# A hybrid decoder step: the decode rows' products with their states and memory values as plain f32 on four 32-column groups, in place of two-part products

## The chip, the cores and the metric

One Trainium2 chip, one of its eight cores. The metric is the device time of one execution in microseconds (us), from runs of the program on the chip; lower is better. A profile is one further execution taken by the hardware profiler, which lists every instruction of the five engines (TensorE as PE, with its weight loads apart as PEld, VectorE as DVE, ScalarE as ACT, GpSimd as POOL, SyncE as SP, whose queue issues most transfers) with its start and its length.

## The reference, cut to what matters

One layer of a decoder trunk for two groups of rows that share all weights: 1024 prompt tokens, and 8 decode rows (one token each) that come with a state. Three mixers read the same normalised stream: an mLSTM, a pooling mixer and an attention to a memory of 256 rows. Everything is f32.

```python
# mLSTM, decode rows: 8 rows x 4 heads, each with a matrix memory C of 256 x 256
num = einsum('btsh,bshd->bthd', s, vc) + inter[..., None] * einsum('bthd,bhde->bthe', qc, C)
C_new = decay[..., None, None] * C + einsum('bshd,bshe->bhde', kw, vc)
...
# attention to the memory, decode rows: each row has its own 256 keys and values per head
s = einsum('blhd,bmhd->bhlm', q, mk) * 256 ** -0.5
p = softmax(s)
o = einsum('bhlm,bmhd->blhd', p, mv)
```

For each of the 8 decode rows and 4 heads there is a product of one row q (1 x 256) with C (256 x 256), and one of the softmax row p (1 x 256) with the row's own values mv (256 x 256). These 64 small products are what the change is about. Nothing is shared between them, so each state and each block of values goes through TensorE once.

## The kernel before, in words

**Precision.** The large products (prompt and decode rows together, 1032 columns) are made in `float32r`, a form of f32 that TensorE multiplies with fewer bits. To keep f32 accuracy, each factor is split in two parts, hi and lo, of 12 bits each: ACT copies it to hi, DVE (or POOL) subtracts hi from it to get lo, and three products (hi·hi, lo·hi, hi·lo) are added in PSUM. `split_part` (L174 to L181) does this for weights, `halves` (L656 to L663) for data; `product` (L665 to L670) makes the three products.

**Order of the work.** Nothing is scheduled by a tool: the order in which the Python code emits instructions is the order on each engine. `run_units` (L186 to L268) goes through a list of units, one for 128 output features, each with three chunks of 384, 384 and 264 token columns (`CHUNKS`); every matmul of it comes from L250. After each 0.6 us (`GRAIN`) of its estimate of such matmuls it splits the next weights (`tick`) and lets the side work advance (`Side.advance`). Side work stands in two lanes of generators; a generator yields the time, in us of large products, that should pass before its next step. So small products are put into the stream of large ones, and the amount of large work between a step that prepares an operand and the step that multiplies it is set by a `yield`.

**Buffers.** `H(...)` takes one of 21 SBUF tiles of 128 x 1032 f32, used in rotation, for nearly all rows and loads; `K1(...)` one of 9 smaller ones; `PS()` one of 5 PSUM banks.

**The state products** are `g_sample_mlstm` (L791 on), in lane 1. There are 16 steps `j`, each with two decode rows `b`, `b + 1` of head `h = j // 4`. A step:
- `load_C(j + 1)` issues the next two states (256 KB each) on SP, and every second time the values `vb`;
- `halves` splits the two states here into two `Ch` tiles: two ACT copies (L659) and two DVE subtractions (L660) of 128 x 512;
- `yield 2.0`;
- 8 matmuls at L878 into one PSUM tile `pq`. The stationary operand is a block of 40 columns of `Qm`, zero but for the decode row's own column: column b holds q's hi part, column 32 + b its lo part. The moving operand is 256 columns of the state's hi or lo part. (2 rows) x (2 halves `k` of the 256 rows) x (2 parts) makes 8;
- the new state: for each row and half an ACT product (L884) and a DVE multiply-add in place on the state `ct` (L885), then two stores on SP (L888);
- after a head's fourth step, rows 0-7 and 32-39 of `pq` are added (L891, L892) and stored into `qC`, and `fill` (L835) puts the next head's q into `Qm`.

**The memory products** are `g_sample_xattn(h)` (L1017 on), one per head, also in lane 1. The scores are made on DVE (L1048) row by row. The softmax is transposed (L1065) and put into `Pm`, with its two parts, in blocks of 16 columns (L1068, L1069). Then, in a loop of 5, two decode rows at a time: `halves` splits the values `tiles[4 + j]` (`ck`) into two `Ch` tiles, `yield 2.0`, and 8 matmuls at L1086 into `po`. The result is copied (L1089), transposed (L1093) and its two parts are added (L1095, L1098).

**Where they lie.** The state steps are put among the large products of the query projection and the output gates, and among the prompt's attention (`g_xattn`, lane 0); the four heads of memory products follow, up to the products with `w_x_out`.

Of the kernel before, what the change touches and what calls it, by code (L numbers as in the profile page):

```python
# [15 lines left out]
T = 1024  # L16
# [14 lines left out]
# Weights are loaded up to EARLY pieces ahead at the start; each piece is split in PARTS steps, not closer  # L31
# together than SHARE of a unit's length, nor sooner than AGE after its load.
# [4 lines left out]
# Time, in us, between two looks at the side work.  # L37
# [51 lines left out]
class Split:  # L89
    """Weights, k-tiles of 128 rows and some columns, as two parts of 12 bits each, whose sum is the weight."""  # L90
# [16 lines left out]
def tile_hybrid_step(ctx: ExitStack, tc: tile.TileContext, x_prompt, mem_prompt, x_sample, cache_mem_k,  # L107
# [43 lines left out]
    # The tensor engine's clock rises after some microseconds of work: until the first loads are here.  # L151
# [9 lines left out]
    # ---------------------------------------------------------------- dense products  # L161
# [11 lines left out]
    def split_part(s, k):  # L173
        """One of the PARTS shares of the k-tiles."""  # L174
# [8 lines left out]
    def run_units(first_loads):  # L183
# [10 lines left out]
        def load_more(first=0):  # L194
            """Loads as far as the buffers reach."""
            while len(here) < len(order):
                n = len(here)
                s = order[n]
                if n < first or n < min(split + 2, free + NW + 1) or s.early and n < split + EARLY:
                    load(s)  # L200
                    here[n] = clock
                else:
                    break

        def tick(us, force=False):
            """Splits, a part at a time, as far as the buffers of the units before reach."""
# [67 lines left out]
    def weight_pairs(w2d, c0, ncols, k0=0, nk=8):  # L274
        """[(Split, column)] for each 128 columns of w2d[k0*128:, c0:c0+ncols]."""
# [12 lines left out]
    # ---------------------------------------------------------------- vectors as columns  # L288
# [59 lines left out]
    # ---------------------------------------------------------------- layer norms  # L348
# [5 lines left out]
    def ln_stats(parts, n):  # L354
        """Mean and 1/deviation of the rows that parts hold side by side."""
# [21 lines left out]
    def to_features(rows, c0, n, g0, b0, wait, per=1):  # L377
        """Transposes normalised rows of one chunk, applies gain and offset, splits into xhi, xlo."""
# [15 lines left out]
    def g_rows_in():  # L394
        """x, normalised, by token."""
# [26 lines left out]
    # ================================================================ phase 1: memory keys and values  # L422
# [43 lines left out]
    def g_kv_rows():  # L466
        """Keys and values by memory row, for the outputs and as the second factor of the attention."""
# [46 lines left out]
    # ================================================================ phase 2: gates of the mLSTM  # L514
    # Per token of a tile: a, exp(-m), exp weight of the state, decay; by head. Tile 8: decode rows.
# [10 lines left out]
    class GateSplit:  # L526
        """Both parts of the gates' weights side by side, each multiplied with both parts of x."""
# [20 lines left out]
    def g_gates():  # L548
# [19 lines left out]
        # b: sum of lf within a tile of 128 tokens; mt: running max.  # L568
# [56 lines left out]
    # ================================================================ phase 3: mLSTM  # L625
# [30 lines left out]
    def halves(hi, lo, src, scale=None):  # L656
        """src, scaled by a column, as two parts of 12 bits each."""
# [7 lines left out]
    def product(out, w, x, first=True, last=True):  # L665
        """out (+)= w^T x, both in two parts."""
# [124 lines left out]
    def g_sample_mlstm():  # L791
        """The decode rows: one step of the recurrence for each of the 32 states."""
# [900 lines left out]
```

## Time and profile before

| | us |
|---|---|
| median of 3 runs | 2214.84 |
| lowest and highest run | 2213.61, 2218.53 |
| span of the profiled execution, first to last instruction | 2210.3 |
| PE busy | 2169.0 |
| DVE busy | 1207.6 |
| ACT busy | 826.1 |
| POOL busy | 364.5 |

The profiled execution has no time of its own beside its span. How to read the views: a matmul's record is longer than the time by which it holds up the next one, since matmuls run one into the other; the cost of a matmul in a stream is the distance from its start to the next start. The shape `128*40 128x256` is 128 rows of a stationary operand with 40 columns, and a moving operand of 256 columns. In a timeline, "x8" is eight instructions merged in one row. What stands in brackets, or behind the second bar, is the time in which the engine had nothing running before the instruction, and what ended it. A group of the kind "who waited for it" lists the engines that stood idle until an instruction on the named tile was done.

### The profile page before, as it was taken

To read this page: it belongs to the slowest core of one execution; us is meant where nothing else is said; L and a number is where in the kernel's file an instruction comes from. 1 tells how busy PE (TensorE), PEld (TensorE's weight loads), DVE (VectorE), ACT (ScalarE), POOL (GpSimd) and SP (SyncE) were. 2 spreads that over 40 slices of the span, in tenths; PEclk is the share of its full clock that TensorE was granted. 3 is DMA by queue.
4 is the path that set the end of the run, shared out by engine and by line. 5 is a ranking of instruction groups with operands and counts; after the bars stand their busy time and mean duration, and the time that the engine had idled before them with its cause. 6 is when DMAs were issued, how large, how long until landed. Compare 5 with 4: busy or idle time off the path is not lost.

```text
span 2210.3 us, 36109 instructions
## 1 busy us (share of the span) xinstructions
PE 2169.0 (98%) x14337; PEld 2140.7 (97%) x14337; DVE 1207.6 (55%) x2776; ACT 826.1 (37%) x1635; POOL 364.5 (16%) x523
## 2 busy tenths in 40 slices
PE   8999999999999999999999999999999999999996
PEld 7899999999999999999999999999999999999996
DVE  6834738383767765635335556644544343443457
ACT  4524343434457543442213333444142341423421
POOL 6301010101110000211004734101010010101104
PEclk9999999999999999999999999999999999999998
DMA  9131232223367664649653223311111111111112
GB/s 264 55 106 53 58 72 53 63 61 70 90 187 260 193 193 159 217 173 339 189 165 103 87 77 86 87 49 49 42 45 49 49 49 48 39 52 45 49 49 77
DMA packets 267795, 229.50 MB, mean 104 GB/s; under 512 B 15669, under 2 KB 245863, under 8 KB 267611
## 3 DMA queue, kind: packets, MB, share of 16 engines
q1 hardware_dynamic: 261291, 208.12, 31.4%
q0 software_dynamic: 6336, 19.09, 2.3%
q8 instruction: 112, 1.84, 0.3%
q14 instruction: 56, 0.46, 0.1%
HBM read 177.13 MB, written 50.64 MB: 103 GB/s over the span
## 4 chain that ended last, share of the span: by engine, by line
PE 88%; DVE 4%; issue 3%; DMA 1%; SPq 1%; ACT 1%; POOL 1%; ACTq 0%; DVEq 0%; POOLq 0%
PE pd L250 79%; PE ps L668 1%; PE ps L669 1%; PE ps L670 1%; DMA Cs<-in_state_C_dram 1%; SPq L171 1%; DVE xlo L387 1%; PE ps L692 1%; PE ps L1086 1%; PE ps L878 1%; PE ps L382 0%; DVE st L358 0%; DVE xhi L386 0%; DVE wlo L181 0%; PE ps L688 0%
## 5 line engine op out<-in xcount | busy, mean ns | idle before, releaser
L250 PE MATMUL pd<-xhi,whi 128*128 128x384 f32 (+1 forms) x2784 | 897.3, 322 | 0.6 <-ACT gf L541 0.6
L250 PE MATMUL pd<-xlo,whi 128*128 128x384 f32 (+1 forms) x2784 | 895.0, 321 | 0.0
L250 PE MATMUL pd<-xhi,wlo 128*128 128x384 f32 (+1 forms) x2784 | 891.2, 320 | 0.0
L250 PEld LDWEIGHTS pd<-xhi,whi 128*128 128x128 f32 x2784 | 524.5, 188 | 1.9 <-ACT gf L541 0.8
L250 PEld LDWEIGHTS pd<-xlo,whi 128*128 128x128 f32 x2784 | 524.9, 189 | 0.1
L250 PEld LDWEIGHTS pd<-xhi,wlo 128*128 128x128 f32 x2784 | 524.3, 188 | 0.0
L181 DVE TENSOR_TENSOR wlo<-raw,whi 128x512 fp32r<-128x512 f32 (+1 forms) x326 | 227.0, 730 | 437.2 <-ACT whi L180 430.6
L180 ACT ACTIVATE whi<-raw 128x512 fp32r<-128x512 f32 (+1 forms) x382 | 219.4, 620 | 271.6 <-PE pd L250 201.4
L1490 ACT ACTIVATE hup<-pd 128x384 f32<-128x384 f32 (+1 forms) x132 | 60.4, 458 | 277.9 <-PE pd L250 277.7
L1503 DVE SCALAR_TENSOR_TENSOR cv<-hup,colB,cv 128x1023 f32<-128x1023 f32 x88 | 112.7, 1281 | 1.6
L1544 DVE TENSOR_TENSOR z<-pd,z 128x384 f32<-128x384 f32 (+3 forms) x120 | 59.5, 511 | 82.6 <-PE pd L250 82.6
L1500 POOL COPY tl<-hup 128x10 f32<-128x10 f32 x44 | 8.4, 192 | 519.6 <-ACT hup L1490 519.6
L366 POOL TENSOR_TENSOR rs<-rs,half 128x1 f32<-128x1 f32 (+2 forms) x60 | 38.0, 633 | 340.2 <-DVE rs L365 330.1
L1491 ACT ACTIVATE cv<-pd,colB 128x384 f32<-128x384 f32 (+1 forms) x132 | 83.6, 633 | 0.0
L181 POOL TENSOR_TENSOR wlo<-raw,whi 128x512 fp32r<-128x512 f32 x56 | 76.3, 1386 | 41.4 <-ACT whi L180 41.4
L1117 POOL DMA_DIRECT2D gD<-ch x60 | 32.8, 547 | 293.5 <-ACT ch L1116 274.4
L1509 POOL TENSOR_TENSOR cv<-cv,cv 128x1032 f32<-128x1032 f32 x22 | 53.1, 2414 | 112.6 <-DVE cv L1503 97.0
L250 PE MATMUL pd<-mh,whi 128*128 128x392 f32 (+2 forms) x192 | 62.7, 326 | 0.6 <-ACT mh L1338 0.6
L250 PE MATMUL pd<-ml,whi 128*128 128x392 f32 (+2 forms) x192 | 61.8, 322 | 0.1
L250 PE MATMUL pd<-mh,wlo 128*128 128x392 f32 (+2 forms) x192 | 61.5, 321 | 0.0
L1116 ACT ACTIVATE ch<-pd,colA 128x384 f32<-128x384 f32 (+1 forms) x60 | 32.7, 545 | 67.1 <-PE pd L250 56.2
L662 ACT ACTIVATE hh<-ps,colA 128x128 fp32r<-128x128 f32 x64 | 23.1, 360 | 79.7 <-DVE hh L663 75.0
(731 smaller groups left out, 4040.9 us busy)
## 6 DMA issues: line engine op xcount, KB each, us to landing
raw<-in_w_in_dram SPq DMA_DIRECT2D x72, 512.0 KB
raw<-in_w_up_dram SPq DMA_DIRECT2D x44, 512.0 KB
raw<-in_w_down_dram SPq DMA_DIRECT2D x22, 512.0 KB
raw<-in_w_o_dram SPq DMA_DIRECT2D x18, 512.0 KB
mx<-mixD SPq DMA_DIRECT2D x16, 516.0 KB
raw<-in_w_mem_kv_dram SPq DMA_DIRECT2D x16, 512.0 KB
Cs<-in_state_C_dram SPq DMA_DIRECT2D x32, 256.0 KB
out_dram<-Cs SPq DMA_DIRECT2D x32, 256.0 KB
```

Source lines behind the costliest of these rows:

```text
L180: nc.scalar.activation(s.hi[:, ks], s.raw[:, ks], AF.Copy)
L181: (nc.gpsimd if s.pool else nc.vector).tensor_sub(s.lo[:, ks], s.raw[:, ks], raw_f(s.hi[:, ks]))
L250: nc.tensor.matmul(p[:u.m, :n], lhsT=a, rhs=b, start=j == 0, stop=j == len(seq) - 1)
L366: nc.gpsimd.tensor_tensor(out=rs[:n], in0=rs[:n], in1=half[:n], op=OP.pow)
L662: nc.scalar.activation(hi, src, AF.Copy, scale=scale)
L1116: nc.scalar.activation(t[:, :n], p[:, :n], AF.Identity, bias=bias)
L1117: nc.gpsimd.dma_start(GD[b][f][:, c0:c0 + n], t[:, :n])
L1490: nc.scalar.activation(rw[:, c0:c0 + n], p[:, :n], AF.Copy)
L1491: nc.scalar.activation(cc[:, c0:c0 + n], p[:, :n], AF.Identity, bias=colB[:, 132 + ft:133 + ft], scale=colB[:, 88 + ft:89 + ft])
L1503: nc.vector.scalar_tensor_tensor(a, b[0], b[1], a, op0=OP.mult, op1=OP.add)
L1509: nc.gpsimd.tensor_mul(cc, CA.pop(j), cc)
L1544: nc.vector.tensor_add(Z2[f][:, cs], p[:, :n], Z2[f][:, cs])
```

## The change

Both kinds of small product are made from the f32 values themselves, with no parts.

- A step takes the decode rows `r` and `r + 4` (`i` = 0, 1) in place of two neighbours.
- Its four products (2 rows x 2 halves `k`) are plain f32 matmuls with a stationary operand of 4 columns, each zero but for the row's own. Each writes to 4 PSUM rows of its own, at 32 * (2 i + k): 0, 32, 64 and 96. A matmul's PSUM rows are the columns of the array that it uses, so the four stand on four groups of 32 columns. Over the four steps of a head each group adds up its own half of 4 decode rows.
- The moving operand is the loaded state or the loaded values, read directly: the `Ch` tiles and their splits are gone, and the DVE update of the state in place comes after the matmuls that read it.
- The halves `k` are added at the end: an ACT copy and a DVE addition of 4 rows, twice, where there was one of 8 rows (states), or a DVE copy of 16 rows (values). The transposes of the values' result are four of 4 rows in place of two of 16.
- `Qm` and `Pm` shrink to 64 columns, and lose the subtractions that made the lo parts. The values `vb` come by two transfers in place of one. The loop of the memory products has 4 passes in place of 5.
- All else is the same; the other lines of the diff take out comments.

The core of the diff:

```diff
-        Qt = H("Qm", F32R)
-        nc.gpsimd.memset(raw_f(Qt), 0.0)
-        Qm = Qt[:, :640].rearrange("p (k b j) -> p k b j", k=2, b=8)
+        Qt = H("Qm")
+        nc.gpsimd.memset(Qt[:, :64], 0.0)
+        Qm = Qt[:, :64].rearrange("p (k i x) -> p k i x", k=2, i=2)
 
         def fill(h):
             for k in range(2):
-                q = smpT[:, 0, k, h * 8:(h + 1) * 8]
-                hi, lo = Qt[:, k * 320:k * 320 + 288:41], Qt[:, k * 320 + 32:(k + 1) * 320:41]
-                nc.vector.tensor_copy(hi, q)
-                nc.vector.tensor_sub(lo, q, raw_f(hi))
+                nc.vector.tensor_copy(Qm[:, k, :, 0:16:5],
+                                      smpT[:, 0, k, h * 8:(h + 1) * 8].rearrange("p (i r) -> p i r", i=2))
...
-            h, b = j // 4, 2 * (j % 4)
+            h, r = divmod(j, 4)
             ct = Ct.pop(j)
-            if b == 0:
+            if r == 0:
                 pq = PS()
-            parts = []
+            yield 2.0
+            for k in range(2):
+                for i in range(2):
+                    o = 32 * (2 * i + k)
+                    nc.tensor.matmul(pq[o:o + 4, :256], lhsT=Qm[:, k, i, 4 * r:4 * r + 4], rhs=ct[:, i, k],
+                                     start=r == 0, stop=r == 3)
             for i in range(2):
-                t = H("Ch", F32R)
-                t = [t[:, p * 512:(p + 1) * 512].rearrange("p (k v) -> p k v", k=2) for p in range(2)]
-                halves(*t, ct[:, i])
-                parts.append(t)
-            yield 2.0
-            for i in range(2):
-                for k in range(2):
-                    for x in range(2):
-                        nc.tensor.matmul(pq[0:40, :256], lhsT=Qm[:, k, b + i], rhs=parts[i][x][:, k],
-                                         start=b + i + k + x == 0, stop=b + i == 7 and k + x == 2)
...
-            if b == 6:
-                t = K1(8)
-                nc.scalar.activation(t, pq[32:40, :256], AF.Copy)
-                nc.vector.tensor_add(t, pq[0:8, :256], t)
-                nc.sync.dma_start(qC[h * 8:(h + 1) * 8], t)
+            if r == 3:
+                for i in range(2):
+                    t = K1(4)
+                    nc.scalar.activation(t, pq[64 * i + 32:64 * i + 36, :256], AF.Copy)
+                    nc.vector.tensor_add(t, pq[64 * i:64 * i + 4, :256], t)
+                    nc.sync.dma_start(qC[h * 8 + 4 * i:h * 8 + 4 * i + 4], t)
...
-        for j in range(5):
-            parts = []
-            if j < 4:
-                if j < 2:
-                    load(cache_mem_v, j + 2)
+        for j in range(4):
+            if j < 2:
+                load(cache_mem_v, j + 2)
+            yield 2.0
+            for m in range(2):
                 for i in range(2):
-                    t = H("Ch", F32R)
-                    t = [t[:, x * 512:(x + 1) * 512].rearrange("p (m v) -> p m v", m=2) for x in range(2)]
-                    halves(*t, tiles[4 + j][:, i])
-                    parts.append(t)
-            yield 2.0
-            for i, t in enumerate(parts):
-                b = 2 * j + i
-                for m in range(2):
-                    for x in range(2):
-                        nc.tensor.matmul(po[0:16, :256], lhsT=Pm[:, m, b * 16:(b + 1) * 16], rhs=t[x][:, m],
-                                         start=b + m + x == 0, stop=b == 7 and m + x == 2)
-        o16 = K1(16)
-        nc.vector.tensor_copy(o16, po[0:16, :256])
+                    o = 32 * (2 * i + m)
+                    nc.tensor.matmul(po[o:o + 4, :256], lhsT=Pm[:, m, i, 4 * j:4 * j + 4], rhs=tiles[4 + j][:, i, m],
+                                     start=j == 0, stop=j == 3)
+        tiles.clear()
+        o4 = []
+        for i in range(2):
+            t = K1(4)
+            nc.scalar.activation(t, po[64 * i + 32:64 * i + 36, :256], AF.Copy)
+            nc.vector.tensor_add(t, po[64 * i:64 * i + 4, :256], t)
+            o4.append(t)
```

TensorE's order at the third state step, in the kernel before (L250 are large products into `pd`, L878 the state products, a row for each of the two decode rows' four):

```order
L250 MATMUL pd_7771<-xlo,whi_7411 128x384
L250 MATMUL pd_7771<-xhi,wlo_7412 128x384
L878 MATMUL ps_7577<-Ch_7759,Qm_6502 40x256 x4
L878 MATMUL ps_7577<-Ch_7762,Qm_6502 40x256 x4
L250 MATMUL pd_7771<-xhi,whi_7411 128x384
L250 MATMUL pd_7771<-xlo,whi_7411 128x384
```

And in the changed kernel, where the state products stand at L873:

```order
L250 MATMUL pd_7745<-xlo,whi_7409 128x384
L250 MATMUL pd_7745<-xhi,wlo_7410 128x384
L873 MATMUL ps_7576<-Cs_7643,Qm_6502 4x256 x4
L250 MATMUL pd_7745<-xhi,whi_7409 128x384
L250 MATMUL pd_7745<-xlo,whi_7409 128x384
```

The four stand at the place of the eight, between the same two large products, and read the loaded state `Cs` in place of its parts `Ch`.

VectorE's order at the same step, before (L660 makes the lo parts `Ch` of the state, L181 those of the next weights; L968 to L976 is the prompt's softmax and its split of the next queries, L885 the state's update):

```order
L660 TENSOR_TENSOR Ch_7759<-Cs_7654,Ch_7759 128x512
L660 TENSOR_TENSOR Ch_7762<-Cs_7654,Ch_7762 128x512
L181 TENSOR_TENSOR wlo_7768<-raw_7556,whi_7767 128x512 x2
L968 TENSOR_REDUCE mx_7790<-ps_7782 128x1
L969 TENSOR_SCALAR mx_7790<-mx_7790 128x1
L953 CAST k_1359_7794<-xq_1067_6223 128x128
L954 TENSOR_TENSOR k_1359_7794<-xq_1067_6223,k_1359_7794 128x128
L953 CAST k_1360_7797<-xq_1106_6429 128x128
L954 TENSOR_TENSOR k_1360_7797<-xq_1106_6429,k_1360_7797 128x128
L975 RECIPROCAL mx_7688<-mx_7688 128x1
L976 TENSOR_SCALAR k_1337_7687<-k_1337_7687,mx_7688 128x256
L885 SCALAR_TENSOR_TENSOR Cs_7654<-Cs_7654,decS,k_1361_7814 128x256
```

And changed (L964 to L972 the same softmax and split, L880 the update):

```order
L181 TENSOR_TENSOR wlo_7742<-raw_7555,whi_7741 128x512 x2
L964 TENSOR_REDUCE mx_7764<-ps_7756 128x1
L965 TENSOR_SCALAR mx_7764<-mx_7764 128x1
L949 CAST k_1353_7768<-xq_1067_6223 128x128
L950 TENSOR_TENSOR k_1353_7768<-xq_1067_6223,k_1353_7768 128x128
L949 CAST k_1354_7771<-xq_1106_6429 128x128
L950 TENSOR_TENSOR k_1354_7771<-xq_1106_6429,k_1354_7771 128x128
L971 RECIPROCAL mx_7672<-mx_7672 128x1
L972 TENSOR_SCALAR k_1333_7671<-k_1333_7671,mx_7672 128x256
L880 SCALAR_TENSOR_TENSOR Cs_7643<-Cs_7643,decS,k_1355_7784 128x256
```

The two `Ch` rows are gone; the update stands where it stood, behind the same softmax, and now also waits for the matmuls that read the state.

More of the change, by code (lines that the diff above doesn't have):

```diff
@@ L880, in g_sample_mlstm @@
-            for i in range(2):
-                r = 2 * j + i
+            yield 2.0
[4 more added lines that the diff above has]
+                                     start=r == 0, stop=r == 3)
+            for i in range(2):
+                x = 8 * h + r + 4 * i
                 for k in range(2):
                     t = K1()
-                    nc.scalar.activation(t, vb[j // 2][:, r % 4], AF.Copy, scale=kwT[:, k, r:r + 1])
-                    nc.vector.scalar_tensor_tensor(ct[:, i, k], ct[:, i, k], decS[:, r:r + 1], t, op0=OP.mult,
+                    nc.scalar.activation(t, vb[j // 2][:, 2 * i + r % 2], AF.Copy, scale=kwT[:, k, x:x + 1])
+                    nc.vector.scalar_tensor_tensor(ct[:, i, k], ct[:, i, k], decS[:, x:x + 1], t, op0=OP.mult,
@@ L1012, in g_xattn @@
             yield 2.2
-    Pm = cp.tile([128, 2, 128], F32R, name="Pm")
+    Pm = cp.tile([128, 2, 2, 16], F32, name="Pm")
     def g_sample_xattn(h):
@@ L1044, in g_sample_xattn @@
             for i in range(2):
[L1045 removed]
+                b = j + 4 * i
                 for m in range(2):
                     scr = K1()
[L1048 removed]
+                    nc.vector.scalar_tensor_tensor(scr, t[:, i, m], 1.0, qb[i][:, j], op0=OP.mult,
                                                    op1=OP.mult, accum_out=sc[:, m, b:b + 1])
@@ L1066, in g_sample_xattn @@
         for m in range(2):
[L1067 to L1069 removed]
+            nc.vector.tensor_copy(Pm[:, m, :, 0:16:5], p[:, m * 8:(m + 1) * 8].rearrange("p (i r) -> p i r", i=2))
         po = PS()
[L1071 to L1089 removed]
+        for j in range(4):
[3 more added lines that the diff above has]
+            for m in range(2):
+                for i in range(2):
+                    o = 32 * (2 * i + m)
[3 more added lines that the diff above has]
+        o4 = []
+        for i in range(2):
+            t = K1(4)
+            nc.scalar.activation(t, po[64 * i + 32:64 * i + 36, :256], AF.Copy)
+            nc.vector.tensor_add(t, po[64 * i:64 * i + 4, :256], t)
+            o4.append(t)
         yield 2.0
@@ L1092, in g_sample_xattn @@
         for k in range(2):
-            nc.tensor.transpose(p[:, k * 16:(k + 1) * 16], o16[:, k * 128:(k + 1) * 128], ident[:16, :16])
-        q = sp.tile([128, 2, 16], F32, tag="ot", name=nm("ot"))
-        nc.vector.tensor_copy(q, p[:, :32].rearrange("p (k c) -> p k c", k=2))
+            for i in range(2):
+                nc.tensor.transpose(p[:, k * 8 + 4 * i:k * 8 + 4 * i + 4], o4[i][:, k * 128:(k + 1) * 128], ident[:4, :4])
         for k in range(2):
             a, b = OT[h][k]
-            nc.vector.tensor_add(q[:, k, 0:8], q[:, k, 0:8], q[:, k, 8:16])
-            nc.vector.tensor_copy(a[:, T:], q[:, k, 0:8])
-            nc.vector.tensor_sub(b[:, T:], q[:, k, 0:8], raw_f(a[:, T:]))
+            nc.vector.tensor_copy(a[:, T:], p[:, k * 8:k * 8 + 8])
+            nc.vector.tensor_sub(b[:, T:], p[:, k * 8:k * 8 + 8], raw_f(a[:, T:]))
         yield 1.0
@@ L1180, in tile_hybrid_step @@
     xq_units(0)
-    on(units[n0], "before", lambda: (nc.gpsimd.memset(raw_f(Pm), 0.0), side.add(1, "smlstm", g_sample_mlstm())))
+    on(units[n0], "before", lambda: (nc.gpsimd.memset(Pm, 0.0), side.add(1, "smlstm", g_sample_mlstm())))
     on(units[-1], "after", lambda: attend(0))
```

18 lines of the change are left out of this document (7 added, 11 removed).

## The prediction

> **What bounds the kernel now.** First the head of the page and its table of busy time, then the granted clock by slices:
>
> ```profile
> span 2210.3 us, 36109 instructions
> ...
> PE 2169.0 (98%) x14337; PEld 2140.7 (97%) x14337; DVE 1207.6 (55%) x2776; ACT 826.1 (37%) x1635; POOL 364.5 (16%) x523
> ...
> PEclk9999999999999999999999999999999999999998
> ```
>
> TensorE is busy for 98% of the span at full clock; no other engine comes near. So a change is worth what it does to TensorE's own time, plus what it takes from TensorE's waits. Second, the two stretches in which the changed products lie, by busy time (length, then PE, PEld, DVE, ACT, POOL, clock, DMA share, GB/s):
>
> ```profile
> 635.00:740.00 105.00, 104.43 (x726) 101.90 (x725) 85.22 (x232) 74.62 (x174) 7.02 (x13) 1.00 0.81 260
> 780.00:960.00 180.00, 177.42 (x1206) 169.44 (x1205) 106.82 (x372) 75.52 (x176) 21.58 (x40) 1.00 0.55 178
> ```
>
> The first holds the 16 state steps, the second the 16 memory steps. PE is recorded idle for 0.57 + 2.58 = 3.15 us there, although DVE is at 81% of the first. Third, who waits for the split tiles `Ch`, with the cost of the splits (min/median/max in ns):
>
> ```profile
> L659 ACT ACTIVATE Ch<-Cs x32: 613/622/634, 639.4 to 735.1; 128x512 fp32r<-128x512 f32 x32
> L660 DVE TENSOR_TENSOR Ch<-Cs,Ch x32: 681/685/695, 640.0 to 735.8; 128x512 fp32r<-128x512 f32 x32
> L659 ACT ACTIVATE Ch<-ck x32: 613/622/635, 784.2 to 952.8; 128x512 fp32r<-128x512 f32 x32
> L660 DVE TENSOR_TENSOR Ch<-ck,Ch x32: 682/685/694, 785.2 to 953.8; 128x512 fp32r<-128x512 f32 x32
> ...
> who waited for it (us, times):
> ...
>   PEld ps L1086: 5.1, 10
> ...
>   PE ps L1086: 2.6, 7
>   PEld ps L878: 2.2, 6
> ...
>   PE ps L878: 0.5, 2
> ```
>
> So 64 ACT copies (64 x 0.622 = 39.8 us) and 64 DVE subtractions (64 x 0.685 = 43.8 us) run beside TensorE, and TensorE's recorded wait for them is 2.6 + 0.5 = 3.1 us: nearly all of the 3.15 us. Nothing more than this wait can be won by taking work from ACT and DVE.
>
> **What a group of eight costs now.** Two groups in TensorE's timeline, one of each kind, with their neighbours (start, length, line, tiles, shape):
>
> ```profile
> 653.94 0.34 PE L250 MATMUL pd<-xhi,wlo 128*128 128x384 f32 x1
> 654.11 1.10 PE L878 MATMUL ps<-Ch,Qm 128*40 128x256 f32 x8
> 655.05 0.34 PE L250 MATMUL pd<-xhi,whi 128*128 128x384 f32 x1
> ```
>
> ```profile
> 853.59 1.09 PE L1086 MATMUL ps<-Ch,Pm 128*16 128x256 f32 x8
> 854.52 0.34 PE L250 MATMUL pd<-xhi,whi 128*128 128x384 f32 x1
> ```
>
> From start to next start 0.94 and 0.93 us, so 0.117 us for one with 256 columns. All 32 groups: 32 x 0.94 = 30.1 us without waits.
>
> **What a group of four will cost.** Plain f32 products with 128 columns stand in the prompt's mLSTM, at L692:
>
> ```profile
> 191.30 0.61 PE L692 MATMUL ps<-q,k 128*128 128x128 f32 x4
> 191.75 0.38 PE L694 MATMUL ps<-ident,o 128*128 128x128 f32 x2
> ```
>
> The code issues two of them there, the trace shows four: a plain f32 matmul is two records, each with its own weight load. Four take 0.45 us, 0.1125 us each for 128 columns, while a `float32r` product takes 0.117 for 256. A record thus passes its columns about twice, if it is the columns that count and not the weight load. That can be told apart at L616, plain f32 with the same weight load and only 8 columns:
>
> ```profile
> 150.38 0.95 PE L616 MATMUL ps<-R,ident 128*128 128x8 f32 x8
> 151.19 0.37 PE L250 MATMUL pd<-xhi,whi 128*128 128x264 f32 x1
> ```
>
> Eight take 0.81 us, 0.10 us each: the floor of the weight load, below 0.1125. I take the columns as the bound, so 256 columns are 0.225 us a record (if the load were the bound at L692, 0.117, as above). A step has four matmuls, eight records. One after another they take 8 x 0.225 = 1.80 us. All four side by side on their four groups of columns, they take as long as one: 2 x 0.225 = 0.45 us. No row of this trace has two matmuls on different groups of columns, so these are the two ends. Between them I take the following: the rows of every timeline start in the order of the program, so the second record of a matmul, which needs the columns that its first still uses, holds back all behind it; once it starts, the first record of the next matmul, on other columns, starts with it. That makes first, second with first, second with first, second with first, second: five slots, 5 x 0.225 = 1.125 us. Against 0.94 that is +0.185 us a step, 32 x 0.185 = +5.9 us. The value is nearer to the group of today than to either end, and it is an assumption on the array, not a reading.
>
> The Trainium skill, "TensorE: Matmul & The Clock Gate", section "Part 3: Packing small matmuls — row/col tiling", says that matmuls on different column groups run together, some 4 ns apart, and that starts and ends keep the program's order; no run here shows either yet. By its formula for the span alone, one matmul and 3 x 4 ns, the sum would go by the lower end; by its rule of order it would go by five slots.
>
> **What goes with the splits.** TensorE's wait for them. The first group of the second head of memory products shows it at its worst:
>
> ```profile
> 840.34 0.63 PE L1086 MATMUL ps<-Ch,Pm 128*16 128x256 f32 x4
> 841.27 0.29 PE L1086 MATMUL ps<-Ch,Pm 128*16 128x256 f32 x1 [0.30 <-ACT Ch L659]
> 841.99 0.52 PE L1086 MATMUL ps<-Ch,Pm 128*16 128x256 f32 x3 [0.44 <-DVE Ch L660]
> 842.35 0.34 PE L250 MATMUL pd<-xhi,whi 128*128 128x384 f32 x1
> ```
>
> The group takes 842.35 - 840.34 = 2.01 us in place of 0.94: 1.07 us lost, where the brackets say 0.74. Each wait hides about 0.16 us more, because a record is 0.28 long and the next could have started after 0.117. The nine waits above make 3.1 + 9 x 0.16 = 4.5 us; the weight loads' own idle time, 5.1 + 2.2 = 7.3 us, is the other bound. I take -5.0 us. What is late next, once no split stands between load and product, is the load itself. It was waited for by ACT, little, as the list of what the engines waited for before working on the states says:
>
> ```profile
> its engine sat idle before it (us, times) until:
> ...
>   DMA Cs<-in_state_C_dram: 3.0, 3
> ```
>
> Three times in 32, and TensorE comes to the states later than ACT did, so I count 0 for it, and 3.0 us if that cover is gone.
>
> **The rest.** The transposes of the memory result become four in place of two, per head. Two take 0.22 us, start to next start:
>
> ```profile
> 803.30 0.29 PE L1093 MATMUL ps<-ident,k 16*128 16x16 f32 x2
> 803.52 0.44 PE L250 MATMUL pd<-xhi,whi 128*128 128x384 f32 x1
> ```
>
> Two more in each of four heads: 8 x 0.11 = +0.9 us. The state's update on DVE (four instructions a step) now waits for the matmuls that read the state, and behind it in DVE's queue stand the next lo parts of weights and the prompt's softmax, which TensorE needs. But for the group at 654.11 the update came only here:
>
> ```profile
> 656.89 1.67 DVE L885 SCALAR_TENSOR_TENSOR Cs<-Cs,decS,k 128x256 f32<-128x256 f32 x4
> ```
>
> That is 1.84 us after the old group's end at 655.05; the longest new group, 1.80 us from 654.11, ends at 655.91, and DVE has lost 2 x 0.685 us of work ahead of it, so it may come to the update at 655.5 and stand for 0.4 us. The large products run on meanwhile: 0, and at most 16 x 0.4 = 6.4 us in the case of 1.80 us if nothing covered it. SP's stores wait for the update and hold back the next state's load behind them; they move with the update, so no later than before. The additional ACT copies and DVE additions at a head's end, the second transfer of `vb` and the shorter clearing on POOL are beside 39.8 and 43.8 us taken from ACT and DVE: 0. ACT's and DVE's relief itself is worth 0 beyond the wait, since TensorE has no other recorded idle time there.
>
> Sum against the span of 2210.3: +5.9 - 5.0 + 0.9 = +1.8 us, 2212.1. The median of the runs stands 4.5 us above the span (2214.84 - 2210.3), and I carry that over: 2216.6 us. A difference under 0.2%, 4.4 us, is about what a measurement of this kernel can't tell from none.
>
> **The rivals.**
>
> *All four side by side.* The second record does not hold back the next matmul: 0.45 us a step. (0.45 - 0.94) x 32 = -15.7, with -5.0 and +0.9: -19.8 us, 2195.0. For it: the array's column groups have outputs and weights of their own, and nothing in the rows says that a started record must end before a third begins. Against it: the start in program order in every timeline. The span formula of the Trainium skill ("TensorE: Matmul & The Clock Gate", "Part 3: Packing small matmuls — row/col tiling") would give this; no trace here bears it out or refutes it for plain f32, which is two records.
>
> *One after another.* Groups of columns do not overlap in plain f32, whose moving values may fill the path that all groups share: 1.80 us a step. (1.80 - 0.94) x 32 = +27.5, with -5.0 and +0.9: +23.4 us, 2238.2, slower. For it: no row shows an overlap at all, and every two products in this trace are a full distance apart. Against it: all of them use the same columns. It decides against the kernel from 0.94 + (5.0 - 0.9) / 32 = 1.07 us a step on.
>
> *TensorE waits for the loads itself.* Five slots, and the 3.0 us that ACT waited come to TensorE: +4.8 us, 2219.6. For it: DMA is at 81% in the first stretch. Against: three waits in 32, at an earlier place.
>
> If a plain record of 256 columns takes only 0.117 us, eight in a row are today's 0.94 and the sum is -5.0 + 0.9 = -4.1 us; that lies inside the range.
>
> **How the numbers follow.** Five slots 0.46, all side by side 0.28, one after another 0.22, the loads 0.04. The likeliest case's own range is 2212 to 2224: the wait between 3.1 and 7.3 us (+1.9 to -2.3), and a sixth slot, 0.225 x 32 = +7.2 us, if the overlap is not complete. Of its 0.46 I put 0.05 below -4.4 us, 0.28 within, 0.13 above; of the loads' 0.04 half is within and half above. Faster: 0.28 + 0.05 = 0.33. Same: 0.28 + 0.02 = 0.30. Slower: 0.22 + 0.13 + 0.02 = 0.37. Either outer case holds more than 2 in 10, so the range takes in both, with 2 us at each end for the wait's bounds: 2193 to 2240.
>
> **What would show it.** In the changed kernel's timeline, the distance from the start of a group at L873 or L1072 to the next large product: 1.1 us for five slots, 0.45 for all side by side, 1.8 for one after another; and whether the starts inside a group fall in pairs, all at once, or evenly. TensorE's idle time in the two stretches should fall from 3.15 us to near 0, with no row in which a group waits for a load of `Cs` or `ck`. The groups of ACT and DVE should lose 39.8 and 43.8 us. I am wrong on the size if the distance is far from 1.1 us, and wrong on the mechanism if the time moves where the distance does not.

## The result, and the profile after

The changed kernel takes 2203.41 us (median of 4 runs, 2202.02 to 2204.46), the kernel before 2215.62 in the runs beside it: ratio 0.9943, 95% interval 0.9931 to 0.9955, so 0.6% faster. The forecast was 2216.6, by its own words too near the time before to tell from it; its chances put slower first (0.37), then faster (0.33), then no change (0.30). The range of 2193 to 2240 held the time.

The page of the changed kernel, busy times and clock:

```profile
span 2200.3 us, 35980 instructions
...
PE 2159.7 (98%) x14345; PEld 2118.7 (96%) x14345; DVE 1170.9 (53%) x2692; ACT 797.5 (36%) x1583; POOL 362.1 (16%) x523
...
PEclk9999999999999999999999999999999999999998
```

The span is 10.0 us shorter. This profiled execution took 2202.02 us, so 1.7 us lie around its span. In the other runs it is some 1.7 to 3.0 us. So the profiled execution of before, with its span of 2210.3, took some 2212 to 2213 us by estimate, at the low end of that kernel's runs; that may be why the medians differ by 12.2 and the traces by 10.0. What follows accounts for the 10.0.

The two stretches by busy time, and then a group of four in the timeline, the one that stands where the group at 654.11 stood:

```profile
635.00:740.00 105.00, 104.00 (x746) 93.11 (x745) 68.88 (x206) 60.81 (x149) 7.15 (x14) 1.00 0.87 264
...
780.00:960.00 180.00, 179.98 (x1258) 166.79 (x1257) 87.97 (x332) 63.26 (x154) 22.71 (x42) 1.00 0.53 176
```

```profile
655.10 0.34 PE L250 MATMUL pd<-xlo,whi 128*128 128x384 f32 x1
655.27 0.33 PE L250 MATMUL pd<-xhi,wlo 128*128 128x384 f32 x1
655.53 0.61 PE L873 MATMUL ps<-Cs,Qm 128*4 128x256 f32 x8
656.08 0.45 PE L250 MATMUL pd<-xhi,whi 128*128 128x384 f32 x1
656.37 0.34 PE L250 MATMUL pd<-xlo,whi 128*128 128x384 f32 x1
```

The group takes 656.08 - 655.53 = 0.55 us to the next large product, where 1.125 was forecast. But two distances are longer than the usual 0.175 between large products: 655.27 to 655.53 is 0.26, and 656.08 to 656.37 is 0.29 (0.09 and 0.11 us more). The same rows, asked for in windows of 0.1 us, show how the eight records start:

```profile
655.53 0.40 PE L873 MATMUL ps<-Cs,Qm 128*4 128x256 f32 x4
655.75 0.40 PE L873 MATMUL ps<-Cs,Qm 128*4 128x256 f32 x4
```

Four records start within 20 ns (at 0, 7, 14 and 20 ns), four more 216 ns after them (216, 223, 230, 236). The last four end their columns another 216 ns on, at 0.45 us, and the next large product starts 0.09 us after that. TensorE's weight loads of the group:

```profile
655.10 0.19 PEld L250 LDWEIGHTS pd<-xhi,wlo 128*128 128x128 f32 x1
655.53 0.11 PEld L873 LDWEIGHTS ps<-Cs,Qm 128*4 128x4 f32 x8 [0.24 <-issue]
656.08 0.19 PEld L250 LDWEIGHTS pd<-xhi,whi 128*128 128x128 f32 x1 [0.43 <-issue]
```

All eight loads start within 0.03 us, two for each matmul in turn: those of the first matmul's two records at 655.531 and 655.536, of the second's at 655.537 and 655.542. (The first and the third of the eight are the ones that wait for a semaphore, one for each of the two states.) So the first matmul's second record stands in the program ahead of the second matmul's first, and yet starts 209 ns after it. A record waits for its own group of columns; what is behind it, on other groups, goes past. And the loads are not made ahead: before the change they began with the last large product (at 653.94 for the group at 654.11), now the weight loader stands for 0.24 us before the group and 0.43 us after its loads.

Who waits for the loaded states `Cs` (for the loaded values `ck` TensorE waits nowhere; before the splits went, it waited 3.1 us by the records for `Ch`):

```profile
who waited for it (us, times):
  DVE Cs L880: 4.2, 4
...
  PE ps L873: 1.0, 1
```

```profile
641.62 0.59 PE L873 MATMUL ps<-Cs,Qm 128*4 128x256 f32 x2
643.21 0.61 PE L873 MATMUL ps<-Cs,Qm 128*4 128x256 f32 x6 [1.00 <-DMA Cs<-in_state_C_dram]
643.75 0.44 PE L250 MATMUL pd<-xhi,whi 128*128 128x384 f32 x1
```

One wait is left, at the very first group: its second state lands 1.6 us after its first matmul, and the group takes 2.13 us in place of 0.55.

For the account I call a visit what a group costs in all: from the start of the last large product before it to the start of the second one after it, less the usual distance after each of the two large products between (0.175 us with 384 columns, 0.122 with 264, 0.117 with 256). Counted off the timelines, all 16 visits of each kind:

| us | states | values | median visit |
|---|---|---|---|
| before | 16.5 | 19.1 | 0.94 |
| changed | 13.4 | 11.9 | 0.74 |

Together -10.3 us: 32 x (0.74 - 0.94) = -6.4 for the group itself; before, the waits on top of 32 x 0.94 made 35.6 - 30.1 = 5.5, which are gone; the one new wait makes +1.6. The transposes of the values' result, to the next large product, take 0.34 us for four in three heads and 0.52 in the first, where two took 0.22: +0.6. That makes -9.7. The same large product starts 0.65 us later than in the trace of before at 640 us, 2.5 earlier at 740, 2.6 at 780, 8.6 earlier at 960, 9.2 at 1200, 10.4 at 1500 and 10.2 at 2180. From 640 to 1200 us that is 9.9 us. The rest is outside: the first 0.65 is left of the start-up, and about 1.2 us between 1300 and 1500 is in a stretch that the change does not touch.

### The profile page after: what moved, and what is told of

It reads as the page before. It is cut to its first block, busy times and chain, and to the rows that moved or that the text cites. A ratio compares the mean times of both kernels' runs of the same rounds, so it can differ in the third digit from the quotient of the medians.

```text
span 2200.3 us, 35980 instructions
## 1 busy us (share of the span) xinstructions
PE 2159.7 (98%) x14345; PEld 2118.7 (96%) x14345; DVE 1170.9 (53%) x2692; ACT 797.5 (36%) x1583; POOL 362.1 (16%) x523
## 4 chain that ended last, share of the span: by engine, by line
PE 87%; DVE 4%; issue 4%; POOL 3%; DMA 1%; ACT 1%; SPq 0%; POOLq 0%; ACTq 0%; DVEq 0%
PE pd L250 78%; PE ps L669 2%; PE ps L668 1%; PE ps L670 1%; POOL ps L1276 1%; DVE xlo L387 1%; PE ps L692 1%; DMA Cs<-in_state_C_dram 1%; PE ps L382 0%; DVE xhi L386 0%; PE ps L873 0%; PE ps L1072 0%; DVE st L358 0%; DMA x<-in_x_prompt_dram 0%; POOL mx L1325 0%
## 5 line engine op out<-in xcount | busy, mean ns | idle before, releaser
L250 PE MATMUL pd<-xhi,whi 128*128 128x384 f32 (+1 forms) x2784 | 898.7, 323 | 0.7 <-ACT gf L541 0.7
L250 PE MATMUL pd<-xlo,whi 128*128 128x384 f32 (+1 forms) x2784 | 894.6, 321 | 0.0
L250 PE MATMUL pd<-xhi,wlo 128*128 128x384 f32 (+1 forms) x2784 | 891.1, 320 | 0.0
L250 PEld LDWEIGHTS pd<-xhi,whi 128*128 128x128 f32 x2784 | 523.8, 188 | 10.3 <-issue 8.3
L250 PEld LDWEIGHTS pd<-xlo,whi 128*128 128x128 f32 x2784 | 524.2, 188 | 1.8 <-issue 1.7
L250 PEld LDWEIGHTS pd<-xhi,wlo 128*128 128x128 f32 x2784 | 523.6, 188 | 1.8 <-issue 1.7
L181 DVE TENSOR_TENSOR wlo<-raw,whi 128x512 fp32r<-128x512 f32 (+1 forms) x326 | 227.0, 731 | 440.7 <-ACT whi L180 432.7
L181 POOL TENSOR_TENSOR wlo<-raw,whi 128x512 fp32r<-128x512 f32 x56 | 76.3, 1386 | 41.7 <-ACT whi L180 41.7
L250 PE MATMUL pd<-mh,whi 128*128 128x392 f32 (+2 forms) x192 | 62.6, 326 | 0.6 <-ACT mh L1327 0.6
L250 PE MATMUL pd<-ml,whi 128*128 128x392 f32 (+2 forms) x192 | 62.0, 323 | 0.1
L250 PE MATMUL pd<-mh,wlo 128*128 128x392 f32 (+2 forms) x192 | 61.5, 320 | 0.0
```

Of the source, the lines that this page charges most:

```text
L181: (nc.gpsimd if s.pool else nc.vector).tensor_sub(s.lo[:, ks], s.raw[:, ks], raw_f(s.hi[:, ks]))
L250: nc.tensor.matmul(p[:u.m, :n], lhsT=a, rhs=b, start=j == 0, stop=j == len(seq) - 1)
```

## The experiments

My theory now was: the four groups of columns work side by side, each with its own line of waiting records; a visit has a fixed cost of going in and out beside that; and the splits' waits are a gain of their own. The rivals were that plain f32 with few stationary columns is cheap by itself, that relief of ACT and DVE won the time, and the prediction's own rule that a waiting record holds back all behind it.

### All four on one group of columns

```diff
-                    o = 32 * (2 * i + k)
-                    nc.tensor.matmul(pq[o:o + 4, :256], lhsT=Qm[:, k, i, 4 * r:4 * r + 4], rhs=ct[:, i, k],
-                                     start=r == 0, stop=r == 3)
+                    nc.tensor.matmul(pq[0:8, :256], lhsT=Qm[:, k, r + 4 * i], rhs=ct[:, i, k],
+                                     start=r + k + i == 0, stop=r == 3 and k + i == 2)
```

The values likewise. `Qm` and `Pm` get blocks of 8 columns, zero but for the row's own, and the additions of halves become one copy.

> Plain f32 without splits as in the changed kernel, but the four matmuls of a step all write the same PSUM rows 0-7, so they stand on one group of columns (a stationary operand of 8 columns, zero but for the row's own; no addition of halves at the end). Theory 'side by side' (each group of columns works by itself, a record waits only for its own group): the distance from a step's first matmul to the next large product goes from the changed kernel's 0.545 to 4 x 0.43 + 0.1 = 1.8 us, the time up by 32 x 1.28 = 41 us on the changed kernel's 2203.4, to about 2244. Rival 'few columns are cheap' (a plain f32 matmul with 4 or 8 stationary columns is short by itself): distance 0.55, time 2203 as changed. The start of the first matmul after the last large product tells on the way in: 0.26 in place of 0.17 us if plain f32 with few columns costs it, 0.17 if the four groups do.

Measured: 2242.24 us, ratio to before 1.0122 (1.0104 to 1.0140). A group in its timeline:

```profile
656.83 0.34 PE L250 MATMUL pd<-xhi,wlo 128*128 128x384 f32 x1
657.10 1.89 PE L871 MATMUL ps<-Cs,Qm 128*8 128x256 f32 x8
658.92 0.44 PE L250 MATMUL pd<-xhi,whi 128*128 128x384 f32 x1
659.20 0.34 PE L250 MATMUL pd<-xlo,whi 128*128 128x384 f32 x1
```

1.82 us, with eight starts 216 ns apart: the same four matmuls cost 3.3 times as much when they share a group. Few columns are not cheap; what made 0.55 of 1.82 is the four groups. This is the cost that the prediction's rival of one after another had, and the kernel loses 27 us by it. The ways in and out are here as well, 0.27 and 0.28 us, so the four groups are not what makes them.

### Two groups, in two orders

```diff
-                    o = 32 * (2 * i + k)
+                    o = 64 * i
...
-                                     start=r == 0, stop=r == 3)
+                                     start=r + k == 0, stop=r == 3 and k == 1)
```

The same with `m` for the values; the additions of halves become copies.

> As the changed kernel, but both halves of a row's product write the same four PSUM rows (two groups of columns in place of four, at rows 0 and 64, no addition at the end). Theory 'side by side': two matmuls in each group one after the other, 2 x 0.43 + 0.1 = 0.97 us a step in place of 0.545, time up by 32 x 0.43 = 14 us to about 2217; the first records of the two groups start within 10 ns of each other, and the second matmul of a group 0.43 us after its first. Theory of the prediction (a record that waits for its own group holds back all behind it): the starts come in slots of 0.216 us, five of them. Rival 'few columns are cheap': 0.55 us, 2203.

Measured: 2216.96 us, ratio 1.0007 (0.9998 to 1.0017). A visit in its timeline, and the records that have started early in it:

```profile
655.76 0.33 PE L250 MATMUL pd<-xhi,wlo 128*128 128x384 f32 x1
656.02 1.03 PE L873 MATMUL ps<-Cs,Qm 128*4 128x256 f32 x8
656.98 0.44 PE L250 MATMUL pd<-xhi,whi 128*128 128x384 f32 x1
...
656.02 0.39 PE L873 MATMUL ps<-Cs,Qm 128*4 128x256 f32 x2
```

The visits take 0.96 us to the next large product, with starts at 0, 7, 216, 223, 432, 439, 648 and 655 ns: pairs, four times 216 ns. Five slots of the prediction's rule would have been seen as starts at 0, 216, 223, 439, ...; the second group starts at 7 ns. How long a line may be was tried with the two loops exchanged, so that both matmuls of the first group stand first:

```diff
-            for k in range(2):
-                for i in range(2):
+            for i in range(2):
+                for k in range(2):
```

> The kernel with two groups of columns, its four matmuls in another order: both of the first group, then both of the second, so four records of one group stand in the program ahead of the first of the other. One look at the starts inside a visit. Theory 'a line for each group' (any number of records of one group may stand in line while the next group goes on): starts at 0 and 0.007 us as with the order in turn, 0.96 us a visit, the span within 2 us of that kernel's 2215.5. Rival 'one may wait' (a group holds one record in work and one in line, the third holds back all behind it): the other group starts at 0.22 us, when the first group's second record starts, or later, and a visit takes 0.43 to 0.65 us longer; 32 of them make 14 to 21 us more.

Measured, one run: 2216.48 us, span 2214.8 (2215.5 in the other order). The same two views:

```profile
656.25 0.33 PE L250 MATMUL pd<-xhi,wlo 128*128 128x384 f32 x1
656.51 1.04 PE L873 MATMUL ps<-Cs,Qm 128*4 128x256 f32 x8
657.48 0.44 PE L250 MATMUL pd<-xhi,whi 128*128 128x384 f32 x1
...
656.51 0.39 PE L873 MATMUL ps<-Cs,Qm 128*4 128x256 f32 x2
```

The visit takes 0.97 us, with starts at 0, 13, 216, 229, 432, 445, 647 and 661 ns. The second group starts 13 ns after the first although three more records of the first stand ahead of it. So at least three records wait in a group's line without holding back the next group, and the order of the code cost nothing here.

### The splits kept, read by nothing

```diff
+            parts = []
+            for i in range(2):
+                t = H("Ch", F32R)
+                t = [t[:, p * 512:(p + 1) * 512].rearrange("p (k v) -> p k v", k=2) for p in range(2)]
+                halves(*t, ct[:, i])
+                parts.append(t)
             yield 2.0
```

And likewise for the values.

> The changed kernel, with the splits of states and values still made at their old place on ACT and DVE (64 copies, 64 subtractions) into tiles that nothing reads. Theory 'wait': only TensorE's waiting for the splits cost time, and it doesn't wait for these, so the time stays within 1.5 us of the changed kernel's 2203.4 and TensorE's recorded idle time in the two stretches stays below 1.5 us. Rival 'relief' (ACT and DVE were late for TensorE at other places, and the 40 and 44 us taken from them are what was won): 5 us or more of the gain goes, 2208 to 2214.

Measured: 2206.56 us, ratio 0.9960 (0.9944 to 0.9976), 3.1 us over the changed kernel, between the two expectations. The intervals of the ratios overlap, but each of the four runs lies above each of the changed kernel's. By the traces the two stages lose 1.4 us against the changed kernel (the same large product is 0.4 us late at 640 and 1.8 at 960), and 3.0 us more are lost between 1300 and 1500 us, in the convolution's stage, where the executions of all these kernels differ by up to 3 us. The two stretches:

```profile
635.00:740.00 105.00, 104.57 (x743) 92.72 (x742) 85.08 (x228) 74.65 (x177) 7.07 (x14) 1.00 0.86 259
780.00:960.00 180.00, 179.48 (x1255) 166.36 (x1254) 108.33 (x366) 80.66 (x187) 22.70 (x42) 1.00 0.54 178
```

ACT and DVE are as busy as before the change (85.08 and 108.33 us of DVE; 85.22 and 106.82 before), and TensorE's recorded idle time is 0.43 + 0.52 = 0.95 us. Relief is worth 1.4 us at most where the splits lay, against 5 or more by the rival. Whether the 3.0 us of this trace in the convolution's stage come of it too, or of that stage's own spread, is not shown.

### Parts as before, the products later

```diff
                 parts.append(t)
-            yield 2.0
+            yield 3.0
...
-            yield 2.0
+            yield 1.0
...
+            late, parts = parts, []
...
-            for i, t in enumerate(parts):
-                b = 2 * j + i
+            for i, t in enumerate(late):
+                b = 2 * (j - 1) + i
```

This is an edit of the kernel before: the states' groups of eight stand 1 us of large products later behind their splits, the values' one pass of the loop later.

> The kernel before, parts and all, with each group of eight products put later behind its splits: 3.0 in place of 2.0 us of large products for the states (and 1.0 in place of 2.0 after), one pass of the loop later for the values. Nothing else changes, the matmuls cost what they did. Theory 'wait' (5 us of the gain are TensorE's waits for the splits, whatever the form of the products): 4 to 6 us less than before, a ratio of 0.9975 to 0.998, and groups of 0.94 us throughout. Rival (the waits move to another place, or the change won its time by the matmuls alone): the time of before within 1.5 us.

Measured: 2207.79 us, ratio 0.9964 (0.9951 to 0.9977), 7.7 us less; by the traces 6.1 us of span. The visits sum to 15.0 (states) and 15.4 us (values), 5.3 less than in the kernel before, at 0.94 each:

```profile
635.00:740.00 105.00, 105.00 (x735) 103.91 (x734) 85.65 (x236) 74.57 (x175) 7.01 (x13) 1.00 0.82 259
780.00:960.00 180.00, 179.84 (x1234) 173.10 (x1233) 107.83 (x379) 75.09 (x176) 22.12 (x41) 1.00 0.55 178
```

TensorE's idle time falls from 3.15 to 0.16 us with all splits in place. So about half of what the change won (5.3 of 10.3 us by the visits) was to be had by putting the old products later behind their splits. The 1.3 us more of this trace lie again between 1300 and 1500 us.

### What the way in and out hangs on

```diff
-        Qt = H("Qm")
-        nc.gpsimd.memset(Qt[:, :128], 0.0)
-        Qm = Qt[:, :128].rearrange("p (k b x) -> p k b x", k=2, b=8)
+        Qt = [H("Qm") for _ in range(2)]
+        for q in Qt:
+            nc.gpsimd.memset(q, 0.0)
+        Qm = [q[:, :1024].rearrange("p (b x) -> p b x", b=8) for q in Qt]
...
-                    nc.tensor.matmul(pq[0:8, :256], lhsT=Qm[:, k, r + 4 * i], rhs=ct[:, i, k],
+                    nc.tensor.matmul(pq[:, :256], lhsT=Qm[k][:, r + 4 * i], rhs=ct[:, i, k],
```

This is an edit of the kernel on one group, of the states alone; the values' products keep their 8 columns.

> The kernel with all four plain f32 matmuls on one group of columns, whose state products now have a stationary operand of 128 columns (zero but for the row's own) in place of 8; the memory products stay at 8. One look at the way in and out. Theory 'narrow': the late first start (0.09 us) and the late next large product come with a stationary operand of few columns in plain f32, since its weight load is not made ahead; with 128 columns the first start is 0.175 us after the last large product, as before the change. Rival 'plain f32': they come with every change between the two forms of f32, 0.26 us also here. The four matmuls take 1.74 us either way (columns of the stationary operand cost nothing).

Measured, one run: 2238.38 us. A state visit with 128 stationary columns:

```profile
655.76 0.33 PE L250 MATMUL pd<-xhi,wlo 128*128 128x384 f32 x1
655.93 1.89 PE L872 MATMUL ps<-Cs,Qm 128*128 128x256 f32 x8
657.47 0.53 PE L250 MATMUL pd<-xhi,whi 128*128 128x384 f32 x1
657.83 0.34 PE L250 MATMUL pd<-xlo,whi 128*128 128x384 f32 x1
```

The first start comes 0.17 us after the last large product, as before the change, and the whole visit is 657.83 - 655.76 - 2 x 0.175 = 1.72 us, or 4 x 0.43 and nothing else. In the same run the values' visits, with 8 columns, take 2.02. So a visit's fixed 0.29 us does not belong to plain f32 as such; it comes with 4 or 8 stationary columns, on one group or on four. The 16 and 40 columns of the old `float32r` groups did not have it either: their visits were 0.94 us, eight times 0.117.

But few columns are not the whole condition. The transposes on TensorE are made of f32 values too (one record each, where a plain f32 product is two), and the trace of before has narrow ones of two kinds, two with 16 rows and 128 columns (L1093) and two with 128 rows and 8 columns (L1020):

```profile
803.04 0.33 PE L250 MATMUL pd<-xhi,wlo 128*128 128x384 f32 x1
803.30 0.29 PE L1093 MATMUL ps<-ident,k 16*128 16x16 f32 x2
803.52 0.44 PE L250 MATMUL pd<-xhi,whi 128*128 128x384 f32 x1
803.80 0.34 PE L250 MATMUL pd<-xlo,whi 128*128 128x384 f32 x1
```

```profile
753.47 0.34 PE L250 MATMUL pd<-xhi,whi 128*128 128x384 f32 x1
753.65 0.38 PE L1020 MATMUL ps<-ident,xq 128*8 128x128 f32 x2
753.79 0.42 PE L250 MATMUL pd<-xlo,whi 128*128 128x384 f32 x1
754.04 0.34 PE L250 MATMUL pd<-xhi,wlo 128*128 128x384 f32 x1
```

Those with 16 rows have the same way in and out as the new groups, 0.26 and 0.28 us, and take 0.41 us as a visit; those with 8 columns start after 0.18 us and take 0.22. So few rows bring the cost as well, and few columns in a transpose do not. What single condition lies behind these cases is not shown.

### Fewer visits

The products of two steps in one visit:

```diff
-            for k in range(2):
-                for i in range(2):
-                    o = 32 * (2 * i + k)
-                    nc.tensor.matmul(pq[o:o + 4, :256], lhsT=Qm[:, k, i, 4 * r:4 * r + 4], rhs=ct[:, i, k],
-                                     start=r == 0, stop=r == 3)
+            if j % 2:
+                for n in (r - 1, r):
+                    for k in range(2):
+                        for i in range(2):
+                            o = 32 * (2 * i + k)
+                            nc.tensor.matmul(pq[o:o + 4, :256], lhsT=Qm[:, k, i, 4 * n:4 * n + 4],
+                                             rhs=Ct[4 * h + n][:, i, k], start=n == 0, stop=n == 3)
+            if j:
+                update(j - 1)
```

`update` is the old code for the new state and its stores; the values' products likewise run at every second pass.

> The changed kernel, with the products of two steps put together: eight matmuls (two in each group of columns) at every second step, for states and for values, so 16 visits of TensorE to the four groups in place of 32. Theory 'in and out' (a visit costs its 0.43 us of columns for each matmul that a group makes, and beside that a fixed 0.31 us: the first start is 0.09 late, the next large product starts 0.11 after the last column, and the one after it is 0.11 late): 16 x 0.31 = 5 us less, about 2198.4. Rival (the loss hangs on each matmul, or is hidden elsewhere): no change, 2203.

Measured: 2197.41 us, ratio 0.9920 (0.9903 to 0.9936). A visit of eight matmuls:

```profile
671.36 0.34 PE L250 MATMUL pd<-xlo,whi 128*128 128x384 f32 x1
671.63 1.05 PE L887 MATMUL ps<-Cs,Qm 128*4 128x256 f32 x16
672.60 0.44 PE L250 MATMUL pd<-xhi,wlo 128*128 128x384 f32 x1
672.88 0.34 PE L250 MATMUL pd<-xhi,whi 128*128 128x384 f32 x1
```

0.977 us to the next large product, 0.432 more than for four matmuls, and the way in and out once. The 16 visits sum to 19.7 us where 32 took 25.3: 5.6 less, of which 0.7 is a shorter first wait, and 16 x 0.3 the visits.

### Still fewer, and the first load earlier

The wait at the first visit, alone:

```diff
         load_C(1)
-        yield 8.0
+        yield 12.0
```

> The changed kernel with the first two states loaded 4 us of large products earlier than their first use (12 in place of 8). Theory: the first visit, 2.13 us in the changed kernel with two idle stretches that end with a load of a state, comes down to 0.545, and the time by 1.6 us to 2201.8. Rival (the loads are late because of what is queued ahead on SP, or the later steps wait in its place): no change, 2203.4, with the wait at another step.

Measured: 2201.34 us, ratio 0.9934 (0.9919 to 0.9949). The first visit is as short as the others (0.545 us to the next large product), the states' visits sum to 12.0 us in place of 13.4, and no later visit waits for a load (one, at 720.74 us, loses 0.16 us to the refill of `Qm`). The intervals of the two ratios overlap, so the medians alone do not settle the 2.1 us between them; 1.4 of them stand in the trace. Then both together, with all of a head's values in one visit:

```diff
-            for n in (j - 1, j) if j % 2 else ():
+            for n in range(4) if j == 3 else ():
```

> The kernel with half the visits, the values' products of a head now all in one visit (sixteen matmuls, four in each group), so 8 + 4 visits, and the first two states loaded 4 us of large products earlier than their first use. Theory 'in and out': four visits less at 0.29 us make 1.2 us, and the wait for the first states, 0.87 us in the kernel with half the visits, goes: 2197.4 - 2.0 = 2195.4. Rival (the values' own loads come late once all four are needed at the same time): TensorE waits at the four visits and the time is 2198 or more.

Measured: 2194.37 us, ratio to before 0.9904 (0.9888 to 0.9921): 21 us less than before, and the fastest version here. Its 12 visits sum to 17.6 us, none of them with a wait; a visit with sixteen matmuls:

```profile
844.19 0.28 PE L250 MATMUL pd<-xhi,wlo 128*128 128x264 f32 x1
844.40 1.91 PE L1082 MATMUL ps<-ck,Pm 128*4 128x256 f32 x32
846.24 0.39 PE L250 MATMUL pd<-xhi,whi 128*128 128x264 f32 x1
```

1.84 us, 0.46 for four.

## Why the prediction was wrong

**The step that failed** is the five slots: "the second record of a matmul, which needs the columns that its first still uses, holds back all behind it". It does not. The next group's first record starts 7 ns after this one's, with this one's second record in line, and 13 ns after it with three in line. That step gave +5.9 us; the group itself made -6.4. I had put the value in the middle of two ends, 0.45 and 1.80, on a rule taken from rows in which all products use the same columns, where any rule of waiting looks the same.

**The rival was right in its mechanism and wrong in its size.** All four side by side: 0.45 us was forecast, and the eight records' starts (216 ns between the two rounds, then another 216 ns of columns) make 0.43 + 0.02. But -15.7 us became -6.4, since each visit costs 0.29 us for going in and out, 32 x 0.29 = 9.3 us that no case of the prediction had. The old groups quoted there have none of it. But the transposes quoted under "The rest" have it: with the large products on both sides of them, as shown above, the row of before told of it. The end on the slower side, one after another, is real too: it is what the kernel on one group does, 1.82 us and 2242 us. That the range held the time is no merit of the five slots: it was wide enough for both rivals, and the time lies between two cases of which neither had this sum.

**What one plain f32 costs** was right: two records, each passing its columns twice, 0.225 us forecast and 0.216 measured for 256 columns. So was the reading that the columns and not the weight load are the bound.

**The wait for the splits** was right: -5.0 forecast; 5.5 us were lost on top of 32 visits of 0.94, 5.3 of which go when the old products are only put later. Taking 0.16 us for each wait beyond its recorded idle time was needed: the records show 3.1.

**"What is late next ... is the load itself"** was named and counted at nothing, with 3.0 us if that cover was gone; +1.6 us came, all of it at the first step, where only 8 us of large products stand between load and use. My reason, that TensorE comes to the states later than ACT did, holds for the other 15.

**The transposes** cost +0.6 us, not +0.9: the 0.22 us that two took are 0.08 from the first to the second and 0.14 on to the next large product, and a further one adds 0.06, not 0.11. **The update on DVE** waited for the matmuls four times, 4.2 us in all, longer than the 0.4 us apiece that I allowed, and TensorE did not wait for it. **Relief of ACT and DVE** was put at 0 and is at most 1.4 us where the splits lay; beyond that stage it is open. Their busy time fell by 28.6 and 36.7 us, less than the 39.8 and 43.8 that the record lengths gave: records of one engine overlap (ACT's in the trace of before sum to 916 us, in a busy time of 826), and ACT has 12 more copies.

With the right group and the visit's fixed cost, the prediction's other terms left as they were, the sum would have been -6.4 - 5.0 + 0.9 = -10.5 us on the span, and -10.0 was measured.

Two rules of the Trainium skill bear on this. "TensorE: Matmul & The Clock Gate", section "Part 3: Packing small matmuls — row/col tiling", gives the span of packed matmuls as one matmul and some 4 ns for each further one: the trace agrees in kind, with 7 ns from one matmul to the next, each of them two records. It also says that matmuls start and end in the program's order, all in one line; the starts above differ, and the measurement decides. "TensorEngine Tiling (Array Packing)", section "Key Properties", says that a change of tiling mode drains TensorE. That fits the 0.29 us, which come with 4 or 8 columns and go with 128, and the transposes with few rows; the old groups of 16 and 40 columns in `float32r` and the transposes with 8 columns had no such cost. No view names the mode that a record runs in, so no run here settles whether the drain is the cause.

## What to carry to other kernels

Small independent products in plain f32 belong on different groups of columns: four of them cost 0.45 us where one after another they cost 1.73, and the splits in two parts with their waits fall away. Put as many as the operands allow into one visit, because each visit costs 0.29 us whether it holds four, eight or sixteen; halving the visits won as much again as half the original change. Look first at what TensorE waits for: moving the old products one step later, with no change of arithmetic, gave about half of the gain. And when you read what a small product costs, take in the large products on both sides of it.

## What the runs showed that I had not expected

A group of columns keeps its own line of at least three waiting records, and the two orders of emitting the matmuls that were tried cost the same (0.96 against 0.97 us a visit). Leaving the large products for narrow plain f32 and coming back costs 0.09 us on the way in, 0.09 us after the last column and 0.11 us on the second large product; with 128 stationary columns nothing of it is left in the visit's sum. The same way in and out stood already in the trace of before, at the transposes with 8 or 16 rows. And the distance between a profiled span and the run's time was 1.7 us here, and 1.7 to 3.0 in all runs, so 1.5 us or more of the 4.5 that the prediction carried over from one to the other was the difference between two executions.
